# Stacked low-rank products; residual stream loaded behind the branch outputs of the combination, with more load buffers

## The chip, the cores and the metric

The kernel runs on one core of one Trainium2 chip. TensorE (PE in the profile) multiplies matrices into PSUM, VectorE (DVE), ScalarE (ACT) and GpSimd (POOL) work on tiles in SBUF, SyncE (SP) issues the transfers (DMA). The metric is the time of one execution on the device in microseconds.

## The reference

One layer of an encoder with two branches over two batches of 512 tokens, 1024 wide, all in fp32:

```python
h = _rmsnorm(x, norm_mix_g[l])
gates, p_a, pq, pkv, pkr = _split(h @ w_in[l], IN_SPLITS)
p_a = _token_shift(p_a, shift_mu[l])
y_a = _rwkv7_branch(p_a, decay_w2[l], decay_w0[l], iclr_a2[l], iclr_a0[l], gate_g2[l],
                    k_k[l], k_a[l], r_k[l], gn_g[l], gn_b[l]).astype(x.dtype) @ w_oa[l]
y_b = _mla_branch(pq, pkv, pkr, q_norm_g[l], w_uq[l], kv_norm_g[l], w_ukv[l], cos, sin) @ w_ob[l]
g_a, g_b = jnp.split(jax.nn.sigmoid(gates), 2, axis=-1)
x = x + (g_a * y_a + g_b * y_b) @ w_out[l]
h = _rmsnorm(x, norm_ffn_g[l])
gt, up = jnp.split(h @ w_gu[l], 2, axis=-1)
x = x + (jax.nn.silu(gt) * up) @ w_down[l]
```

and a last norm. In the RWKV branch decay and rate come from low-rank products, per direction, with 64 inner rows, and the output gate from one with 160:

```python
wl = -jax.nn.softplus(-(base + jnp.tanh(lora) @ up)) - 0.5
...
return jax.nn.sigmoid(base + lora @ up)
...
g = jax.nn.sigmoid(pg) @ g2
```

## The kernel before

An fp32 product is three matmuls of a rounded type: `split` (L131) makes from a tile a high part (a cast on ACT) and a low part (a subtraction on DVE), and `mm3` adds up high x high, high x low and low x high in one PSUM tile. Nearly all matmuls have 128 rows and 512 columns (a batch's tokens), and are recorded at L125 by `mm`.

In time the program goes: norm and first projections (0 to 50 us); `lora_phase`, with its projections (50 to 160); the latents of attention; the units of RWKV, four head pairs by two batches by two directions, among projections (200 to 700); attention, with the states of the last units (700 to 940); `combine(0)`, the output product of batch 0, `combine(1)` and the output product of batch 1; the norm, the two feed-forward products (1200 to 1813).

`lora_phase` (L404) projects the four low-rank inputs, shifts them along the tokens into `sh` tiles and splits them into `lw`, `la`, `lg`, `lx` (index 0 high, 1 low). For decay and rate both directions share a tile: 64 rows are the one, 64 the other, and the weights `w2` are zero in the rows of the other direction. Then, for each of four pairs `p` and two batches `b`, four products `lu` (decay and rate, two directions) and one `lug` (the gate, in two parts: 128 rows of `lg`, 32 of `lx`) are made in PSUM tiles `mg` (two buffers). A `lu` is evicted by ACT (L464), scaled by POOL (L466) and stored by SP (L467) from a `lut` tile; a `lug` is copied by DVE (L472) and stored. These five share four `lut` buffers.

`combine(b)` (L1034) loads for each pair first the attention output `o_d` (`e` = 1), then the RWKV output `y_d` (`e` = 0) into `ld` tiles (two buffers). To `y_d` POOL adds `bo_d` (L1045) and DVE multiplies the gate (L1046), both loaded into `bg` tiles. Each is split into `yo`. Then for each of eight column blocks `j` it loads `g_` and, for both branches, the weights `wab` into `raw` (two buffers), splits these, and makes the product `pab` of 12 matmuls; a DVE operation multiplies the gate into it (L1062). `pab001` is block 0, batch 0, branch 1, attention.

The residual stream `x2`, eight tiles of 128 tokens by 1024 (512 KB each), is loaded in `combine_thread` (L1099), when all units are done and batch 0's attention is. It is read in the output product.

Two things set the order. TensorE's order is fixed by `drive`: six threads (states, RWKV outputs, solves, preparation, attention, combination) yield, each with a modelled delay, and the first whose time has come goes on; constants such as `YQ`, `YK`, `YO3`, `YS`, `YG`, `L1`, `L2`, `PL` (from a score tile to its transposes `pt`) and `C0` (from the loads to the first `pab`) are such delays. The orders of the other engines and of SP's queue come from the tile scheduler's own simulation. A tile pool's buffer is free for its next tile when its last reader is done.

Names in attention: `sc` are scores, of batch, head and query block (`sc160`: batch 1, head 6, block 0), `mx` and `pr` their minimum and exponential, `pt` the transposes of `pr`, `pT` their copies, `pav` the product with the values, `rbp` its transposes, `rb` the result stored to `o_d`. `rbp_gn13` are the transposes of the last unit's result, behind which stands its store to `y_d`.

Of the kernel before, what the change touches and what calls it, by code (L numbers as in the profile page):

```python
# [19 lines left out]
NB = 2  # L20
# [18 lines left out]
PSTAG = ("f", NF)  # L39
ALAG = 2  # L40
NSTART = 27
L1 = 0.7
L2 = 0.9
L3 = 1.0
TL = 40
SLACK = 1.4
# [10 lines left out]
YP2 = 3  # L57
YP3 = 1
YP4 = 2.84
YG = 0.7  # L60
YT = 1.43
YT2 = 0.85
YM1 = 2
YM2 = 1.1
YO1 = 1.3
YO2 = 2.11
YO3 = 3.44
YS = 0.5
YQ = 2.18
YK = 1.63  # L70
OFFS = 200000, 150000, 120000, 100000, 0, 0
JP = NFF // 2
NRH = 10
# [3 lines left out]
LATW = 0.2  # L77
HOLDW = 0.7
PRIOW = 1
C0 = 18  # L80
PL = 2.81
HORD = (0, 1)
VQB = 3
HALVES = (4,)
# [20 lines left out]
def trunk(ctx, tc, outs, x, w_in, w2, g2, w_uq, w_ukk, w_ukv, w_oab, w_out, w_gu, w_down,  # L105
# [298 lines left out]
    def lora_phase():  # L404
        with ExitStack() as sl:
            lp = pool(sl, "lora")
            lw = [[lp.tile([P, S], F32R, name=f"lw{b}{i}") for i in range(2)] for b in range(NB)]
            la = [[lp.tile([P, S], F32R, name=f"la{b}{i}") for i in range(2)] for b in range(NB)]
            lg = [[lp.tile([P, S], F32R, name=f"lg{b}{i}") for i in range(2)] for b in range(NB)]
            lx = [[lp.tile([P, S], F32R, name=f"lx{b}{i}") for i in range(2)] for b in range(NB)]  # L410
            tosb = lp.tile([64, S], F32, name="tosb")
            nc.sync.dma_start(tosb, to[0:64])
            for b, ps in enumerate((yield from proj(4, "w"))):
                t = sh(f"shw{b}")
                shifted(t, ps, T_W)
                nc.scalar.activation(t, t, AF.Tanh)
                split(*lw[b], t)
            for b, ps in enumerate((yield from proj(5, "a"))):
                t = sh(f"sha{b}")
                shifted(t, ps, T_A)  # L420
                split(*la[b], t)
            for b, ps in enumerate((yield from proj(6, "g"))):
                t = sh(f"shg{b}")
                shifted(t, ps, T_G)
                nc.scalar.activation(t, t, AF.Tanh, scale=0.5)
                nc.vector.tensor_scalar(t, t, 0.5, 0.5, op0=ALU.mult, op1=ALU.add)
                split(*lg[b], t)
            for b, ps in enumerate((yield from proj(3, "x"))):
                t = sh(f"shx{b}")
                nc.vector.memset(t, 0.0)  # L430
                r = slice(64, 96)
                shifted(t, ps, T_X, r)
                nc.scalar.activation(t[r], t[r], AF.Tanh, scale=0.5)
                nc.vector.tensor_scalar(t[r], t[r], 0.5, 0.5, op0=ALU.mult, op1=ALU.add)
                split(*lx[b], t)
                ta, tb = sh(f"kra{b}")[0:32], sh(f"krb{b}")[0:32]
                nc.vector.tensor_mul(ta, ps[0:32], tosb[0:32])
                nc.vector.tensor_mul(tb, ps[32:64], tosb[32:64])
                nc.vector.tensor_add(ta, ta, tb)
                nc.sync.dma_start(kr_d[b][0:32], ta)  # L440
                nc.sync.dma_start(kr_d[b][32:64], ta)
            w2hi = lp.tile([P, 4, S], F32R, name="w2hi")
            w2lo = lp.tile([P, 4, S], F32R, name="w2lo")
            g2hi = lp.tile([P, 2, S], F32R, name="g2hi")
            g2lo = lp.tile([P, 2, S], F32R, name="g2lo")
            for i in range(4):
                t = lp.tile([P, S], F32, tag="raw", bufs=2, name=f"w2raw{i}")
                nc.sync.dma_start(t, w2[i])
                split(w2hi[:, i], w2lo[:, i], t)
            for i in range(2):  # L450
                t = lp.tile([P, S], F32, tag="raw", bufs=2, name=f"g2raw{i}")
                nc.sync.dma_start(t, g2[i])
                split(g2hi[:, i], g2lo[:, i], t)
            for p in range(NPAIR):
                for b in range(NB):
                    sl_p = slice(p * P, (p + 1) * P)
                    for i in range(4):
                        src = lw if i < 2 else la
                        ps = mg(f"lu{b}{p}{i}")
                        yield from mm3(ps, w2hi[:, i, sl_p], w2lo[:, i, sl_p], src[b][0], src[b][1])  # L460
                        t = lp.tile([P, S], F32, tag="lut", bufs=4, name=f"lut{b}{p}{i}")
                        dst = t[:, ::-1] if i % 2 else t
                        hcol = half[:, i * 4 + p:i * 4 + p + 1]
                        nc.scalar.activation(dst, ps, AF.Tanh, scale=0.5, bias=hcol)  # L464
                        f = -0.5 * KAPPA if i < 2 else 0.5
                        nc.gpsimd.tensor_scalar(t, t, f, f, op0=ALU.mult, op1=ALU.add)  # L466
                        nc.sync.dma_start(rwkv_in[b][p][:, 3 + i], t)  # L467
                    ps = mg(f"lug{b}{p}")
                    yield from mm3(ps, g2hi[:, 0, sl_p], g2lo[:, 0, sl_p], lg[b][0], lg[b][1], stop=False)
                    yield from mm3(ps, g2hi[:, 1, sl_p], g2lo[:, 1, sl_p], lx[b][0], lx[b][1], start=False)  # L470
                    t = lp.tile([P, S], F32, tag="lut", bufs=4, name=f"lugt{b}{p}")
                    nc.vector.tensor_copy(t, ps)  # L472
                    nc.sync.dma_start(rwkv_in[b][p][:, 7], t)
        yield from rkv_tiles(0)
# [559 lines left out]
    def combine(b, cp_, newps, m):  # L1034

        yo = [[cp_.tile([P, NPAIR, S], F32R, name=f"yo{b}{e}{j}") for j in range(2)] for e in range(2)]
        for e in (1, 0):
            for p in range(NPAIR):
                t = cp_.tile([P, S], F32, tag="ld", bufs=2, name=f"ld{b}{e}{p}")
                nc.sync.dma_start(t, (y_d, o_d)[e][b][p])  # L1040
                if e == 0:
                    bg = cp_.tile([P, 2, S], F32, tag="g3", bufs=2, name=f"bg{b}{p}")
                    nc.sync.dma_start(bg[:, 0], bo_d[b][p])
                    nc.sync.dma_start(bg[:, 1], rwkv_in[b][p][:, 7])
                    nc.gpsimd.tensor_add(t, t, bg[:, 0])  # L1045
                    nc.vector.tensor_mul(t, t, bg[:, 1])  # L1046
                split(yo[e][0][:, p], yo[e][1][:, p], t)
        yield C0
        for j in range(KD):
            g_ = cp_.tile([P, 2, S], F32, tag="g3", bufs=2, name=f"g3{j}{b}")  # L1050
            nc.sync.dma_start(g_, gate_d[b][j])
            for e in (1, 0):
                raw = cp_.tile([P, 4 * P], F32, tag="raw", bufs=2, name=f"wab{b}{j}{e}")
                nc.sync.dma_start(raw, w_oab[j][:, e * 512:(e + 1) * 512])
                wt = [cp_.tile([P, 4 * P], F32R, tag=f"w{i}", bufs=2, name=f"wab{b}{j}{e}{i}") for i in range(2)]
                split(*wt, raw)
                ps = newps(f"pab{j}{b}{e}")
                for k in range(NPAIR):
                    ws = slice(k * P, (k + 1) * P)
                    yield from mm3(ps, wt[0][:, ws], wt[1][:, ws], yo[e][0][:, k], yo[e][1][:, k],  # L1060
                                   start=(k == 0), stop=(k == NPAIR - 1))
                nc.vector.scalar_tensor_tensor(out=g_[:, e], in0=g_[:, e], scalar=1.0, in1=ps,  # L1062
                                               op0=ALU.add, op1=ALU.mult)
            nc.gpsimd.tensor_add(g_[:, 0], g_[:, 0], g_[:, 1])  # L1064
            nc.scalar.activation(m[0][:, j], g_[:, 0], AF.Copy, scale=0.5)
            nc.vector.scalar_tensor_tensor(out=m[1][:, j], in0=g_[:, 0], scalar=0.5, in1=m[0][:, j],
                                           op0=ALU.mult, op1=ALU.subtract)
# [23 lines left out]
    def combine_thread():  # L1091
        for i in range(NU):
            yield has("post", i)
        yield has("attn", 0)
        rst_.close()
        x2p = pool(p4, "x2p")
        x2.extend(x2p.tile([P, D], F32, name=f"x2_{t}") for t in range(8))
        for t in range(8):
            nc.sync.dma_start(x2[t], x[t // 4, (t % 4) * P:(t % 4 + 1) * P, :])  # L1099
        mtiles(m0st, 0)  # L1100
        with ExitStack() as s3:
            yield from combine(0, pool(s3, "c30"), mg, mt[0])

    done.add(("rkv", 0))
    drive([(100000, first_prep()), (0, latents(latp))])
# [511 lines left out]
def layout(i):  # L1617
# [21 lines left out]
    r["w_in"] = wt.reshape(len(cols), P, KD * P)  # L1639
    w2 = np.zeros((4, P, 512), f)  # L1640
    for d in range(2):
        w2[d, d * 64:(d + 1) * 64] = a["decay_w2"][0, d]
        w2[2 + d, d * 64:(d + 1) * 64] = a["iclr_a2"][0, d]
    r["w2"] = w2
    g2 = np.zeros((2, P, 512), f)
    g2[0] = a["gate_g2"][0, :128]
    g2[1, 64:96] = a["gate_g2"][0, 128:]
    r["g2"] = g2
    uq = a["w_uq"][0].reshape(2, P, 8, 96)
    even = np.concatenate([np.arange(96), 80 + np.arange(16), 64 + np.arange(16)])  # L1650
# [76 lines left out]
```

## Time and profile before

| | |
|---|---|
| median of three runs | 1813.38 us (1812.76 to 1814.93) |
| the profiled execution | 1814.92 us |
| its span, first to last instruction | 1813.1 us |
| mean granted clock of TensorE | 0.981 |
| DMA moved | 208.96 MB, 115 GB/s over the span |

A row of the profile names the line, the engine, the operation and the tiles (written from read). `x48` counts rows, a bracket `[2.53 <-ACT yo L132]` is the idle time ahead of a row and what ended it. A row of a matmul is longer than the distance to the next, since they run on into each other. The granted clock is a share of full speed.

### The profile page before, as it was taken

How to read it: one execution, taken by the hardware profiler on the slowest of the kernel's cores; microseconds unless marked ns; L12 is line 12 of the kernel's file. 1: busy time of each engine (PE TensorE's matmuls, PEld its weight loads, DVE VectorE, ACT ScalarE, POOL GpSimd, SP SyncE). 2: the span in 40 equal slices, each digit the busy share in tenths (PEclk: the TensorE clock that was granted, in tenths of full speed). 3: DMA queues.
4: the chain of work that ended last, by engine and by line, in shares of the span. 5: the costliest groups of instructions: out<-in, count | busy, mean ns of one | idle time of the engine just before them, and what ended most of it. 6: DMA issues, size and time to landing. Idle time of an engine off the chain costs nothing.

```text
span 1813.1 us, 30886 instructions
## 1 busy us (share of the span) xinstructions
PE 1719.7 (95%) x11708; PEld 1359.8 (75%) x11708; DVE 1074.9 (59%) x1773; ACT 778.1 (43%) x1512; POOL 641.4 (35%) x992
## 2 busy tenths in 40 slices
PE   6999989999999997999999999699999999989997
PEld 5887767767777775666667989488888888868886
DVE  6633555635355455765656557956556555488757
ACT  5534343333444335676653324333333333235445
POOL 3012355363644637261012124843333343100006
PEclk8999999999999998999989999899999999999999
DMA  4354433424343334211266641022223222383442
GB/s 158 121 177 163 130 112 90 120 79 130 104 111 107 90 111 113 76 44 45 82 218 210 210 156 36 24 93 95 97 93 105 81 72 91 99 289 123 128 134 93
DMA packets 185332, 208.96 MB, mean 115 GB/s; under 512 B 102816, under 2 KB 114464, under 8 KB 185184
## 3 DMA queue, kind: packets, MB, share of 16 engines
q1 hardware_dynamic: 184320, 205.48, 35.9%
q8 instruction: 92, 1.51, 0.3%
q10 hardware_dynamic: 720, 0.98, 0.2%
q0 software_dynamic: 144, 0.52, 0.1%
q14 instruction: 56, 0.46, 0.1%
HBM read 147.70 MB, written 59.24 MB: 114 GB/s over the span
## 4 chain that ended last, share of the span: by engine, by line
PE 66%; DVE 10%; DMA 9%; POOL 7%; issue 4%; ACT 3%; SPq 1%; DVEq 0%; POOLq 0%; ACTq 0%
PE pgC L125 10%; PE pgB L125 6%; PE pj_gt L125 6%; PE pgA L125 6%; PE dx L125 5%; PE pj_rkv L125 5%; PE dy L125 3%; POOL lt L847 2%; POOL el L849 2%; PE s L125 2%; PE pab L125 2%; PE pj_mla L125 2%; DMA wor<-in_w_out 2%; PE pwo L125 2%; PE gx L125 2%
## 5 line engine op out<-in xcount | busy, mean ns | idle before, releaser
L847 POOL TENSOR_TENSOR lt<-lane,el 128x126 f32<-128x126 f32 (+22 forms) x248 | 96.7, 390 | 38.8 <-DMA lane<-nt_d 20.4
L849 POOL TENSOR_TENSOR el<-el,lt 128x126 f32<-128x126 f32 (+22 forms) x248 | 98.3, 396 | 19.1
L125 PE MATMUL pab<-yo,wab 128*128 128x512 f32 x384 | 97.2, 408 | 7.0 <-ACT yo L132 2.5
L125 PE MATMUL pj_gt<-h_lo,whi_gt 128*128 128x512 f32 x240 | 99.5, 415 | 0.0
L125 PE MATMUL pj_gt<-h_hi,whi_gt 128*128 128x512 f32 x240 | 99.0, 413 | 0.0
L125 PE MATMUL pj_gt<-h_hi,wlo_gt 128*128 128x512 f32 x240 | 98.4, 410 | 0.3 <-DVE wlo_gt L133 0.3
L125 PEld LDWEIGHTS pab<-yo,wab 128*128 128x128 f32 x384 | 73.1, 195 | 28.0 <-DVE wab L133 5.5
L125 PE MATMUL pwo<-woh,m 128*128 128x256 f32 x512 | 93.6, 283 | 0.0
L1217 POOL TENSOR_TENSOR s<-uraw 128x512 f32<-128x512 f32 x22 | 29.3, 1332 | 150.6 <-DMA uraw<-in_w_gu 141.2
L125 PEld LDWEIGHTS pwo<-woh,m 128*128 128x128 f32 x512 | 80.2, 192 | 0.3
L125 PE MATMUL pj_rkv<-h_hi,wlo_rkv 128*128 128x512 f32 x192 | 77.4, 406 | 1.3 <-DVE wlo_rkv L133 1.3
L125 PE MATMUL pj_rkv<-h_hi,whi_rkv 128*128 128x512 f32 x192 | 77.6, 404 | 0.0
L125 PE MATMUL pj_rkv<-h_lo,whi_rkv 128*128 128x512 f32 x192 | 76.7, 399 | 0.0
L125 PE MATMUL pwo<-wol,m 128*128 128x256 f32 x256 | 72.4, 284 | 0.5 <-DVE wol L133 0.5
L1596 POOL TENSOR_TENSOR x<-x,dp 128x512 f32<-128x512 f32 x4 | 6.3, 1591 | 178.8 <-DVE x L1595 178.8
L1285 DVE TENSOR_TENSOR p<-p,pgC 128x512 f32<-128x512 f32 x22 | 15.1, 687 | 86.9 <-PE pgC L125 86.9
L936 ACT COPY sva<-s 64x128 f32<-64x128 f32 x64 | 16.5, 258 | 98.0 <-PE s L125 83.9
L1064 POOL TENSOR_TENSOR g<-g 128x512 f32<-128x512 f32 x16 | 24.2, 1514 | 92.8 <-DVE g L1062 76.0
L937 DVE COPY svb<-s 64x128 f32<-64x128 f32 x64 | 18.8, 294 | 62.3 <-ACT sva L936 33.9
L466 POOL TENSOR_SCALAR lut<-lut 128x512 f32<-128x512 f32 x32 | 20.2, 634 | 98.7 <-ACT lut L464 98.3
L616 DVE TENSOR_REDUCE mx<-sc 128x1 f32<-128x512 f32 x64 | 43.8, 688 | 18.5 <-PE sc L125 17.9
L125 PEld LDWEIGHTS pj_gt<-h_hi,wlo_gt 128*128 128x128 f32 x240 | 45.1, 188 | 9.2 <-DVE wlo_gt L133 1.0
(1561 smaller groups left out, 5533.7 us busy)
## 6 DMA issues: line engine op xcount, KB each, us to landing
graw<-in_w_gu SPq DMA_DIRECT2D x22, 512.0 KB, 3.5
uraw<-in_w_gu SPq DMA_DIRECT2D x22, 512.0 KB, 3.5
a_d<-a SPq DMA_DIRECT2D x21, 512.0 KB, 3.2
w<-in_w_down SPq DMA_DIRECT2D x42, 256.0 KB, 4.3
x<-in_x SPq DMA_DIRECT2D x16, 512.0 KB, 8.0
rwkv_in<-lut SPq DMA_DIRECT2D x32, 256.0 KB, 2.1
gate_d<-gtt SPq DMA_DIRECT2D x32, 256.0 KB, 2.4
wab<-in_w_oab SPq DMA_DIRECT2D x32, 256.0 KB, 3.5
```

What stands on the lines that cost most here:

```text
L125: pin(nc.tensor.matmul(out, lhsT, rhs, start=start, stop=stop, **kw), n if out.shape[0] > 64 else n / 2)
L466: nc.gpsimd.tensor_scalar(t, t, f, f, op0=ALU.mult, op1=ALU.add)
L616: nc.vector.tensor_reduce(mx, sc, axis=AX.X, op=ALU.min)
L847: eng.tensor_mul(lv, lane[:, s, s + 1:].unsqueeze(1).to_broadcast([P, m_, n]), el[:, 0:m_, s].unsqueeze(2).to_broadcast([P, m_, n]))
L849: eng.tensor_add(ev, ev, lv)
L936: nc.scalar.copy(sva[HA, :, c], s2[HA])
L937: nc.vector.tensor_copy(svb[HB, :, c], s2[HB])
L1064: nc.gpsimd.tensor_add(g_[:, 0], g_[:, 0], g_[:, 1])
L1217: vg(ES[min(j, 1)]).tensor_add(s1, a21, a22)
L1285: nc.vector.tensor_add(p1, p1, x_)
L1596: nc.gpsimd.tensor_add(xs(1, t, 1), xs(1, t, 1), p5[t])
```

## The change

It has three parts. In `lora_phase` high and low part of one direction now stand in the two halves of one tile of 128 rows (`stacked`), the weights' 64 rows are laid out twice, and so one matmul makes high x high and low x high: a `lu` has two matmuls instead of three. The 32 rows of the gate's second part become one tile (`lx`, rows 32 to 127: high, high, low) against one weight tile (`g2x`: low, high, high), and `lug` has four matmuls instead of six. In the combination `ld` gets four buffers, `raw` three, `C0` is 14, and the loads of `x2` are written behind the loads of `combine(0)`. Eight delays get other values.

```diff
-L1 = 0.7
-L2 = 0.9
+L1 = 0.55
+L2 = 1.04
-YG = 0.7
+YG = 0.75
-YO3 = 3.44
-YS = 0.5
-YQ = 2.18
-YK = 1.63
+YO3 = 4.26
+YS = 0.41
+YQ = 2
+YK = 1.72
-C0 = 18
-PL = 2.81
+C0 = 14
+PL = 3.5
...
+            top, bot = slice(0, 64), slice(64, 128)
+
+            def stacked(dst, t):
+                for d, (own, other) in enumerate(((top, bot), (bot, top))):
+                    nc.scalar.copy(dst[d][own], t[own])
+                    nc.vector.tensor_sub(dst[d][other], t[own], dst[d][own])
...
-            lx = [[lp.tile([P, S], F32R, name=f"lx{b}{i}") for i in range(2)] for b in range(NB)]
+            lx = [lp.tile([P, S], F32R, name=f"lx{b}") for b in range(NB)]
...
-                split(*lw[b], t)
+                stacked(lw[b], t)
...
-                split(*la[b], t)
+                stacked(la[b], t)
...
-                split(*lx[b], t)
+                for rows, own in ((slice(0, 32), slice(0, 32)), (r, r), (slice(32, 64), r)):
+                    nc.scalar.copy(lx[b][rows], t[own])
+                nc.vector.tensor_sub(lx[b][96:128], t[r], lx[b][r])
...
-                split(g2hi[:, i], g2lo[:, i], t)
+                if i == 0:
+                    split(g2hi, g2lo, t)
+                else:
+                    nc.scalar.copy(g2x[bot], t[bot])
+                    nc.scalar.copy(g2x[0:32], t[0:32])
+                    nc.vector.tensor_sub(g2x[32:64], t[64:96], g2x[64:96])
...
-                        yield from mm3(ps, w2hi[:, i, sl_p], w2lo[:, i, sl_p], src[b][0], src[b][1])
+                        mm(ps, w2hi[:, i, sl_p], src[b][i % 2], stop=False)
+                        yield 0
+                        mm(ps, w2lo[:, i, sl_p], src[b][i % 2], start=False)
+                        yield 0
...
-                    yield from mm3(ps, g2hi[:, 0, sl_p], g2lo[:, 0, sl_p], lg[b][0], lg[b][1], stop=False)
-                    yield from mm3(ps, g2hi[:, 1, sl_p], g2lo[:, 1, sl_p], lx[b][0], lx[b][1], start=False)
+                    yield from mm3(ps, g2hi[:, sl_p], g2lo[:, sl_p], lg[b][0], lg[b][1], stop=False)
+                    mm(ps, g2x[:, sl_p], lx[b], start=False)
+                    yield 0
...
-                t = cp_.tile([P, S], F32, tag="ld", bufs=2, name=f"ld{b}{e}{p}")
+                t = cp_.tile([P, S], F32, tag="ld", bufs=4, name=f"ld{b}{e}{p}")
...
-                raw = cp_.tile([P, 4 * P], F32, tag="raw", bufs=2, name=f"wab{b}{j}{e}")
+                raw = cp_.tile([P, 4 * P], F32, tag="raw", bufs=3, name=f"wab{b}{j}{e}")
...
-        for t in range(8):
-            nc.sync.dma_start(x2[t], x[t // 4, (t % 4) * P:(t % 4 + 1) * P, :])
         mtiles(m0st, 0)
         with ExitStack() as s3:
-            yield from combine(0, pool(s3, "c30"), mg, mt[0])
+            cg = combine(0, pool(s3, "c30"), mg, mt[0])
+            yield next(cg)
+            for t in range(8):
+                nc.sync.dma_start(x2[t], x[t // 4, (t % 4) * P:(t % 4 + 1) * P, :])
+            yield from cg
...
-        w2[d, d * 64:(d + 1) * 64] = a["decay_w2"][0, d]
-        w2[2 + d, d * 64:(d + 1) * 64] = a["iclr_a2"][0, d]
+        w2[d] = np.tile(a["decay_w2"][0, d], (2, 1))
+        w2[2 + d] = np.tile(a["iclr_a2"][0, d], (2, 1))
...
-    g2[1, 64:96] = a["gate_g2"][0, 128:]
+    g2[1, 64:] = np.tile(a["gate_g2"][0, 128:], (2, 1))
```

In TensorE's order, near the end of `lora_phase`, before (the last `lu` of pair 3, batch 0, and its `lug`):

```order
L125 MATMUL lu033_1073<-la00_385,w2hi_769 128x512
L125 MATMUL lu033_1073<-la01_386,w2hi_769 128x512
L125 MATMUL lu033_1073<-la00_385,w2lo_770 128x512
L125 MATMUL lug03_1081<-lg00_389,g2hi_771 128x512
L125 MATMUL lug03_1081<-lg01_390,g2hi_771 128x512
L125 MATMUL lug03_1081<-lg00_389,g2lo_772 128x512
L125 MATMUL lug03_1081<-lx00_393,g2hi_771 128x512
L125 MATMUL lug03_1081<-lx01_394,g2hi_771 128x512
L125 MATMUL lug03_1081<-lx00_393,g2lo_772 128x512
```

The same place after the change:

```order
L125 MATMUL lu033_1046<-la01_386,w2hi_779 128x512
L125 MATMUL lu033_1046<-la01_386,w2lo_780 128x512
L125 MATMUL lug03_1053<-lg00_389,g2hi_781 128x512
L125 MATMUL lug03_1053<-lg01_390,g2hi_781 128x512
L125 MATMUL lug03_1053<-lg00_389,g2lo_782 128x512
L125 MATMUL lug03_1053<-lx0_393,g2x_783 128x512
```

Three matmuls became two and six became four; `la01` is now the stacked tile of the second direction. TensorE has 48 rows fewer in all.

SP's queue where the residual stream is loaded, before (`x2_4` is its fifth tile, `ld010` the first load of the combination, `wab011` a weight tile, `o_d11` a store of attention):

```order
L1099 DMA x2_4_10374<-in_x 128x1024
L1099 DMA x2_5_10375<-in_x 128x1024
L1099 DMA x2_6_10376<-in_x 128x1024
L1099 DMA x2_7_10377<-in_x 128x1024
L1040 DMA ld010_10398<-o_d00_99 128x512
L575 DMA o_d11_104<-rb11_10363 128x512
L1040 DMA ld011_10402<-o_d01_100 128x512
L1043 DMA bg00_10416<-bo_d00_122 128x512
L1044 DMA bg00_10416<-rwkv_in00_75 128x512
L1054 DMA wab011_10847<-in_w_oab 128x512
L1054 DMA wab010_10867<-in_w_oab 128x512
L1043 DMA bg01_10425<-bo_d01_123 128x512
```

The same positions of the queue after the change:

```order
L1122 DMA x2_4_10287<-in_x 128x1024
L1122 DMA x2_5_10288<-in_x 128x1024
L1059 DMA ld010_10303<-o_d00_99 128x512
L1122 DMA x2_6_10289<-in_x 128x1024
L1122 DMA x2_7_10290<-in_x 128x1024
L1059 DMA ld011_10307<-o_d01_100 128x512
L1073 DMA wab001_10552<-in_w_oab 128x512
L1073 DMA wab000_10676<-in_w_oab 128x512
L1073 DMA wab011_10755<-in_w_oab 128x512
L1059 DMA ld012_10311<-o_d02_101 128x512
L1059 DMA ld013_10315<-o_d03_102 128x512
L1062 DMA bg00_10321<-bo_d00_122 128x512
```

Two of the eight `x2` loads moved behind `ld010`; six still stand ahead of it, although they are written behind it. `wab001` and `wab000`, which stood ahead of `x2_0` before, now stand behind `ld011`, and `o_d11` behind the `ld` loads of branch 1.

TensorE's order at the end of attention, before:

```order
L129 MATMUL pt151_10578<-idn_62,pr151_10515 128x128 x4
L125 MATMUL sc160_10586<-kt100_9626,qh16_10532 128x512
L125 MATMUL sc160_10586<-kt101_9627,qh16_10532 128x512
L125 MATMUL sc160_10586<-kt100_9626,ql16_10533 128x512
L129 MATMUL pt152_10595<-idn_62,pr152_10548 128x128 x4
L125 MATMUL sc161_10601<-kt100_9626,qh16_10532 128x512
L125 MATMUL sc161_10601<-kt101_9627,qh16_10532 128x512
L125 MATMUL sc161_10601<-kt100_9626,ql16_10533 128x512
```

The same place after the change:

```order
L129 MATMUL pt151_10534<-idn_62,pr151_10471 128x128 x4
L125 MATMUL pab001_10558<-yo010_10301,wab0010_10554 128x512
L125 MATMUL pab001_10558<-yo011_10302,wab0010_10554 128x512
L125 MATMUL pab001_10558<-yo010_10301,wab0011_10555 128x512
L125 MATMUL sc160_10562<-kt100_9620,qh16_10488 128x512
L125 MATMUL sc160_10562<-kt101_9621,qh16_10488 128x512
L125 MATMUL sc160_10562<-kt100_9620,ql16_10489 128x512
L129 MATMUL pt152_10571<-idn_62,pr152_10504 128x128 x4
```

The first matmuls of `pab001` moved from behind `sc170` to behind `pt151`. The last row of `pab000`, which reads the last `yo` of batch 0, stood behind `rbp13` before and stands ahead of `pt172` now; ahead of `rbp13` there were 18 rows of `pab` and are 31. Earlier in attention `rbp_gn13` stood behind `pt132` before and stands ahead of `pt130` now.

More of the change, by code (lines that the diff above doesn't have):

```diff
@@ L443, in lora_phase @@
             w2lo = lp.tile([P, 4, S], F32R, name="w2lo")
-            g2hi = lp.tile([P, 2, S], F32R, name="g2hi")
-            g2lo = lp.tile([P, 2, S], F32R, name="g2lo")
+            g2hi = lp.tile([P, S], F32R, name="g2hi")
+            g2lo = lp.tile([P, S], F32R, name="g2lo")
+            g2x = lp.tile([P, S], F32R, name="g2x")
             for i in range(4):
```

## The prediction

> **What bounds the kernel now.** First the page: how busy each engine is, and what the chain that ended last is made of.
>
> ```profile
> PE 1719.7 (95%) x11708; PEld 1359.8 (75%) x11708; DVE 1074.9 (59%) x1773; ACT 778.1 (43%) x1512; POOL 641.4 (35%) x992
> PE 66%; DVE 10%; DMA 9%; POOL 7%; issue 4%; ACT 3%; SPq 1%; DVEq 0%; POOLq 0%; ACTq 0%
> ```
>
> TensorE holds two thirds of the chain, so a matmul taken out counts where TensorE never waits, and elsewhere only as far as what it waits for comes earlier too. 95% is an average, so the two changed stages are read apart, each with the view of busy time by stretches (start:end, length, then busy time and count for PE, PEld, DVE, ACT and POOL, the granted clock, DMA share, GB/s). First the low-rank stage:
>
> ```profile
> 50.00:75.00 25.00, 25.00 (x111) 20.63 (x110) 15.70 (x25) 13.80 (x24) 2.75 (x4) 1.00 0.41 137
> 75.00:100.00 25.00, 25.00 (x111) 20.51 (x111) 16.81 (x25) 9.69 (x16) 2.48 (x4) 1.00 0.36 118
> 100.00:125.00 25.00, 25.00 (x111) 20.49 (x110) 8.45 (x13) 9.70 (x15) 4.47 (x7) 1.00 0.50 156
> 142.00:160.00 18.00, 17.14 (x74) 11.93 (x72) 2.33 (x4) 8.25 (x12) 7.44 (x12) 1.00 0.55 214
> ```
>
> Up to 125 us TensorE is busy all the time, with 111 matmuls of 512 columns in 25 us: **25/111 = 0.225 us from start to start**, at full clock (the 0.39 us of a single row overlaps its neighbours). There a removed matmul is worth its 0.225. From 142 on there are gaps, and the timeline of PE shows their pattern:
>
> ```profile
> 144.19 0.62 PE L125 MATMUL lu<-lw,w2hi 128*128 128x512 f32 x2
> ...
> 145.19 0.72 PE L125 MATMUL lu<-lw,w2hi 128*128 128x512 f32 x2 [0.16 <-DVE lugt L472]
> ...
> 149.16 0.62 PE L125 MATMUL lu<-lw,w2hi 128*128 128x512 f32 x2
> ...
> 154.14 0.61 PE L125 MATMUL lu<-lw,w2hi 128*128 128x512 f32 x2
> ```
>
> The last three blocks stand back to back, one in (154.14 - 144.19) / 2 = 4.98 us, while their 18 matmuls need 18 x 0.225 = 4.05. TensorE waits there for the eviction, through the two `mg` buffers.
>
> The other stage is the start of combine(0). The timeline of PE, rows with a wait ahead of them:
>
> ```profile
> 932.64 0.50 PE L125 MATMUL pab<-yo,wab 128*128 128x512 f32 x1 [0.66 <-DVE yo L133]
> ...
> 942.08 3.23 PE L125 MATMUL pab<-yo,wab 128*128 128x512 f32 x6 [2.53 <-ACT yo L132]
> 945.84 14.42 PE L125 MATMUL pab<-yo,wab 128*128 128x512 f32 x50 [0.54 <-DVE g L1062]
> 961.13 3.06 PE L125 MATMUL pab<-yo,wab 128*128 128x512 f32 x12 [0.87 <-DVE wab L133]
> 964.63 5.25 PE L125 MATMUL pab<-yo,wab 128*128 128x512 f32 x22 [0.45 <-DVE wab L133]
> 970.93 1.45 PE L125 MATMUL pab<-yo,wab 128*128 128x512 f32 x4 [1.05 <-ACT wab L132]
> ```
>
> The waits for `yo` and the gate product come to 0.66 + 2.53 + 0.54 = 3.73 us, those for `wab` to 2.37. Behind the longest the matmuls are also slow: six take 3.23 us and fifty 14.42, where at 0.225 they would take 1.35 and 11.25. The stretches say why:
>
> ```profile
> 940.00:945.00 5.00, 2.92 (x6) 1.78 (x6) 3.87 (x5) 1.79 (x4) 0.83 (x1) 0.64 0.52 170
> 945.00:950.00 5.00, 4.46 (x11) 3.29 (x11) 2.58 (x4) 1.16 (x2) 1.61 (x1) 0.50 0.59 208
> 950.00:955.00 5.00, 5.00 (x20) 4.03 (x19) 3.24 (x6) 2.38 (x4) 0.00 (x0) 0.83 0.95 340
> ```
>
> The granted clock is down to half for about 10 us. That costs (3.23 - 1.35) + (14.42 - 11.25) = 5.05, less about 0.4 for the two row ends that run on: **4.6 us**.
>
> **Why `yo` is late.** Busy transfers of 900 to 915, the residual stream's eight loads (L1099, start of the first and last), and what belongs to the tiles `ld`:
>
> ```profile
> 905.00:910.00 5.00, 5.00 (x28) 4.12 (x27) 2.78 (x5) 3.66 (x11) 0.00 (x0) 1.00 1.03 415
> 910.00:915.00 5.00, 4.21 (x24) 2.99 (x23) 3.83 (x8) 4.89 (x12) 0.00 (x0) 1.00 1.04 398
> ...
> L1099 SPq DMA_DIRECT2D x<-in_x x8: 382/529/924, 898.3 to 902.6; - x8
> ...
> L132 ACT CAST yo<-ld x8: 617/620/632, 915.4 to 942.0; 128x512 fp32r<-128x512 f32 x8
> L133 DVE TENSOR_TENSOR yo<-ld,yo x8: 678/688/693, 916.1 to 942.7; 128x512 fp32r<-128x512 f32 x8
> L1040 SPq DMA_DIRECT2D ld<-o_d x4: 319/320/326, 904.5 to 919.1; - x4
> L1040 SPq DMA_DIRECT2D ld<-y_d x4: 319/320/422, 924.9 to 934.0; - x4
> L1045 POOL TENSOR_TENSOR ld<-ld,bg x4: 1260/1272/1284, 927.7 to 939.6; 128x512 f32<-128x512 f32 x4
> L1046 DVE TENSOR_TENSOR ld<-ld,bg x4: 676/1206/1760, 929.0 to 941.3; 128x512 f32<-128x512 f32 x4
> ...
> DMA to landing us min/median/max: 2.6/4.1/9.6
> ```
>
> The transfers run full (share 1.03) while eight loads of 512 KB, 1.27 us each at 412 GB/s, come ahead of the first `ld`, issued at 904.5 and landed 9.6 us later, about 914.1. With two `ld` buffers the y_d loads then wait for splits of o_d tiles and are issued from 924.9 on; the last split starts at 942.7.
>
> **The change, part by part.**
>
> *Stacked products.* Per pair and batch 18 matmuls become 4 x 2 + 3 + 1 = 12, over eight blocks 48 fewer. 3 x 6 = 18 of these lie in the last three blocks, the other 30 where TensorE is busy all the time (nearly: two in the last `lug` ahead of them): 30 x 0.225 = **6.8 us**. In the last blocks the bound is the eviction, from these rows of the tile `lut`, 140 to 162:
>
> ```profile
> L466 POOL TENSOR_SCALAR lut<-lut x14: 617/619/628, 139.6 to 158.7; 128x512 f32<-128x512 f32 x14
> L467 SPq DMA_DIRECT2D rwkv_in<-lut x14: 319/320/368, 140.2 to 159.3; - x14
> L464 ACT ACTIVATE lut<-lu,half x13: 687/687/698, 139.3 to 157.9; 128x512 f32<-128x512 f32 x13
> ...
> DMA to landing us min/median/max: 2.0/2.0/3.0
> ```
>
> A buffer is held for 0.69 + 0.62 + 2.0 = 3.3 us and some tenths of handing over, say 3.5, a `lugt` (no POOL step) some 2.8; five tiles over four buffers make (4 x 3.5 + 2.8) / 4 = 4.2 a block. I take 4.3. Ends: ACT alone, 4 x 0.69 = 2.75, and no gain, 4.98. So 3 x (4.98 - 4.3) = **2.0 us**, between 0 and 6.7. The stage gives 8.8, between 6.8 and 13.5.
>
> The stacking adds 9 casts on ACT and 4 subtractions on DVE; fewer rows make them no cheaper:
>
> ```profile
> L439 DVE TENSOR_TENSOR kra<-kra,krb 32x512 f32<-32x512 f32 x2 | 1.4, 678 | 0.1
> L132 ACT CAST la<-sha 128x512 fp32r<-128x512 f32 x2 | 1.2, 616 | 0.0
> ```
>
> 9 x 0.62 + 4 x 0.68 = 8.3 us, which I cost at nothing: between 50 and 125 TensorE has projections queued, DVE is idle for at least 8 of each 25 us and ACT for 11. If that cover went, 8.3 would come back and the stage would be 1.5 us worse than none at all on its low end; the rows exclude that while projections stand between the products.
>
> *Loads of the combination.* By SP's order six of the eight residual loads still stand ahead of the first `ld`, not none. What changes: two loads and the two weight loads fewer ahead of it (2 x 1.27 + 2 x 0.64 = 3.8 us), and all of it starts earlier, since `rbp_gn13` now stands ahead of `pt130` instead of behind `pt132`:
>
> ```profile
> 890.22 0.60 PE L129 MATMUL pt<-idn,pr 128*128 128x128 f32 x4
> ...
> 894.61 0.66 PE L129 MATMUL rbp_gn<-idn,rb_gn 128*128 128x128 f32 x4
> ```
>
> That is 4.4 us. So the first `ld` lands near 914.1 - 3.8 - 4.4 = 906 on the old clock, and ACT casts it right behind the exponential of `pr150`, near 909. With four buffers the y_d loads no longer wait for `o_d12`'s store or for splits; I place the first at 914 and, with 4.1 to land, 1.27 for POOL's sum, about 1.2 for the product, twice over for the ring of two `bg` tiles, 0.62 and 0.69 for the split, the last `yo` at 929, instead of 942.7. Its first reader on TensorE stands near 931. So the 3.73 go, and with the long wait the half clock, 4.6. For later `wab`, with three buffers instead of two, I take half of the 2.37: 1.2. Against it: the matmuls of `pab001` stand earlier, behind `pt151`, while `wab001` is now loaded behind the `ld`s; TensorE can wait there, and once more for the last `yo`. Ends: 0 and the 2.53 that it waits today; I take 1.5 for both together, nearer to the long end since the margins are 2 us or less. Queued behind such a wait are `sc160`, `pt152` and `qps17`, hence ACT's copies. **3.73 + 4.6 + 1.2 - 1.5 = 8.0 us**, between 0 (the loads' order decides) and 3.73 + 4.6 + 2.37 = 10.7.
>
> *The constants* move rows in the units by a few places, and in attention put the transposes `pt` about one piece later. TensorE waits there little:
>
> ```profile
> PE pt L129 <- ACT pr L618: 1.7, 4, 0.7
> PE pt L129 <- ACT pT L555: 1.0, 2, 0.8
> ```
>
> 2.7 us in six waits is all that later transposes can win; the same again may be lost. I take 0.
>
> *Sum:* 8.8 + 8.0 = 16.8 us. The profiled execution took 1814.92, so 1798.1; the median of the three runs, 1813.38, lies 1.54 lower, so **1796.6**.
>
> **The rivals.**
>
> *Six loads ahead are as bad as eight* (the change doesn't do what it says). If the earlier start doesn't come about, the first `ld` lands near 910, ACT stands at its cast ahead of `pr151`, and what the y_d side wins is lost to exponentials. For it: SP's order and the share of 1.03. Against: it is y_d, not o_d, that ends last. Only the 8.8 remain: 1804.6.
>
> *The half clock stays.* [...] Then 4.6 of the 8.0 are missing, the sum is 12.2, the time 1801.2. [...]
>
> *More is won:* the last blocks go at ACT's 2.75 (4.7 more) and the 2.7 of `pt` vanish: 1789.2. Against it: the landing of 2.0 us is in the ring.
>
> *Attention stalls (slower).* The new order lets each of the 64 pieces wait once for its exponential or its copy, because the casts of `yo` and `wab` now stand in ACT's queue between them and state rows are moved. The six waits above average 0.45 us; 64 x 0.45 = 29 us, so 1825.4. It decides from 16.8 / 64 = 0.26 us a piece on. Against: transposes stand later, not earlier, and only the last ten pieces share ACT with the casts.
>
> **How the numbers follow.** Forecast 0.62, six loads as bad 0.12, half clock stays 0.14, more 0.06, attention stalls 0.06. A measurement of this kernel tells about 0.2% (3.6 us) from no change. The first four are faster by more: 0.94. Of the stalls 0.04 are slower, 0.02 land within 0.2%. The range goes from 1789.5, near the two upper ends together (13.5 + 10.7 = 24.2, 1789.2), to 1805.5, just beyond the case of the six loads.
>
> **What would show it.** Right: 48 matmuls fewer and `ss_kk` about 8.8 us earlier; blocks of `lu` 4.3 us apart at the end; the last `yo` split about 11 us before the old place, no wait for `yo` over 1 us, clock 1.00 through the start of combine(0). Wrong: TensorE waiting in 50 to 125; a half clock behind a wait for `wab001` or `yo`; many small waits at `pt` or `sc` between 705 and 930; a dip that has moved to the norm ahead of the feed-forward part.

## The result, and the profile after

| | before | after |
|---|---|---|
| median | 1814.16 us (1812.76 to 1816.37, 4 runs) | 1801.62 us (1799.46 to 1804.07, 4 runs) |
| ratio, 95% interval | | 0.9923 (0.991 to 0.9935) |
| the profiled execution | 1814.92 us | 1804.07 us |
| its span, mean clock | 1813.1 us, 0.981 | 1802.3 us, 0.980 |

The kernel became faster by 12.5 us in the medians, 11.8 to 16.3 by the interval of the ratio. The forecast was 16.8 less and 1796.6 us, with a range of 1789.5 to 1805.5. The profiled execution after is the slowest of the four; the other three had clocks of 0.983, 0.981 and 0.983 at 1799.46, 1802.57 and 1800.66 us.

The page after, busy time by engine and the chain:

```profile
PE 1713.5 (95%) x11660; PEld 1353.0 (75%) x11660; DVE 1080.5 (60%) x1777; ACT 784.4 (44%) x1521; POOL 639.8 (35%) x992
PE 69%; DVE 9%; DMA 7%; POOL 6%; issue 6%; ACT 3%; SPq 1%; POOLq 0%; DVEq 0%; ACTq 0%
```

48 matmuls are gone, and the clock is no better. The start of combine(0) after, by the tile `ld` (first and last start) and by stretches (the granted clock is the third number from the end):

```profile
L132 ACT CAST yo<-ld x8: 617/628/647, 906.1 to 928.5; 128x512 fp32r<-128x512 f32 x8
L133 DVE TENSOR_TENSOR yo<-ld,yo x8: 682/690/1726, 907.5 to 930.8; 128x512 fp32r<-128x512 f32 x8
L1059 SPq DMA_DIRECT2D ld<-o_d x4: 326/326/472, 895.7 to 904.1; - x4
L1059 SPq DMA_DIRECT2D ld<-y_d x4: 319/322/326, 909.4 to 918.4; - x4
...
940.00:945.00 5.00, 5.00 (x25) 4.19 (x25) 2.47 (x4) 1.83 (x3) 0.00 (x0) 1.00 0.35 115
945.00:950.00 5.00, 4.82 (x22) 3.65 (x20) 2.52 (x5) 1.51 (x3) 1.61 (x1) 1.00 0.89 271
```

The clock is full where it was half, as forecast, and no row waits for `yo` any more. The times are further from the forecast than they look. Its 909 for the first cast and 929 for the last split were on the clock of before, and attention now begins 6.5 us earlier (first `kps` at 698.7 instead of 705.2). Counted from there, the first cast came 2.8 us earlier than before (207.4 instead of 210.2; 6.4 were forecast) and the last split 5.4 us earlier (232.1 instead of 237.5; 13.7 were forecast). The timeline of PE has one new wait, the one expected at the earlier `pab001`, and later waits for weights and for the gate product:

```profile
911.84 1.31 PE L125 MATMUL pab<-yo,wab 128*128 128x512 f32 x3 [0.85 <-ACT wab L132]
...
950.84 6.09 PE L125 MATMUL pab<-yo,wab 128*128 128x512 f32 x24 [1.02 <-ACT wab L132]
957.50 17.72 PE L125 MATMUL pab<-yo,wab 128*128 128x512 f32 x76 [0.58 <-DVE g L1081]
```

The last blocks of the low-rank stage are what was not forecast. The timeline of PE:

```profile
135.61 0.39 PE L125 MATMUL lu<-lw,w2hi 128*128 128x512 f32 x1
...
139.78 0.44 PE L125 MATMUL lu<-lw,w2hi 128*128 128x512 f32 x1
...
145.13 0.39 PE L125 MATMUL lu<-lw,w2hi 128*128 128x512 f32 x1
...
149.26 0.50 PE L125 MATMUL lu<-la,w2hi 128*128 128x512 f32 x1 [1.64 <-ACT lut L482]
...
151.72 1.70 PE L125 MATMUL ss_kk<-blk2sb,kksq 128*128 128x2 f32 x8
```

They take 4.17, 5.35 and 6.59 us, 16.1 together, where 14.9 stood before and 12.9 were forecast; from 149.8 on the clock is half (0.50) for 6.8 us. The waiting engine is ACT, whose evictions wait for stores to land (timeline of ACT):

```profile
141.79 1.34 ACT L482 ACTIVATE lut<-lu,half 128x512 f32<-128x512 f32 x2 [2.12 <-DMA rwkv_in<-lut]
...
148.53 1.27 ACT L482 ACTIVATE lut<-lu,half 128x512 f32<-128x512 f32 x2 [1.68 <-DMA rwkv_in<-lut]
```

In these blocks before the change, stores issued 0.7 to 1.1 us after each other mostly landed after 2.0 us. After it, five are issued within 2.9 us from 143.2 on (3.6 us or more before), and two of them took 3.65 and 3.61 us, so the ring turned more slowly just when it should turn faster. That closeness alone lengthens them is argued, not shown: other stores, 0.7 to 1.1 us apart, took 2.8 us here.

To see where time went, the span is cut at the starts of the first rows of `pj_a` (the low-rank stage), `gx` (the units), `kps` (attention), `pwo` (the output product) and `nt_f` (norm and feed-forward). Microseconds of the profiled executions, up to the end of the last matmul (the 7.8 to 7.9 us of the span behind it are left out), with three of the experiments below:

| stage | before | after | stack only | buffers only | stack and loads |
|---|---|---|---|---|---|
| ahead of `pj_a` | 42.8 | 41.1 | 41.8 | 42.9 | 42.7 |
| low-rank stage, latents | 155.0 | 152.5 | 148.0 | 155.0 | 148.1 |
| units | 507.4 | 505.3 | 508.8 | 508.3 | 508.6 |
| attention, combine(0) | 286.1 | 280.9 | 283.2 | 277.2 | 276.3 |
| output product to combine(1) | 103.7 | 102.3 | 104.9 | 102.3 | 102.3 |
| from the norm on | 710.2 | 712.5 | 710.0 | 712.5 | 712.5 |

The low-rank stage is 4.5 us longer after the change than with the products alone. In it 13.7 us stand at half clock after and 3.4 with the products alone; half of the difference, 5.1 us by an estimate, would account for it.

### The profile page after: what moved, and what is told of

Read it like the earlier page. It is cut to its first block, busy times and chain, and to the rows that moved or that the text cites. A ratio compares the mean times of both kernels' runs of the same rounds, so it can differ in the third digit from the quotient of the medians.

```text
span 1802.3 us, 30805 instructions
## 1 busy us (share of the span) xinstructions
PE 1713.5 (95%) x11660; PEld 1353.0 (75%) x11660; DVE 1080.5 (60%) x1777; ACT 784.4 (44%) x1521; POOL 639.8 (35%) x992
## 4 chain that ended last, share of the span: by engine, by line
PE 69%; DVE 9%; DMA 7%; POOL 6%; issue 6%; ACT 3%; SPq 1%; POOLq 0%; DVEq 0%; ACTq 0%
PE pgC L125 10%; PE pj_gt L125 8%; PE pgB L125 7%; PE pgA L125 6%; PE dx L125 4%; PE pab L125 4%; PE pwo L125 4%; PE s L125 3%; PE dy L125 2%; PE sc L125 2%; POOL el L868 2%; POOL lt L866 2%; PE pav L125 2%; PE gx L125 2%; PE dz L125 2%
## 5 line engine op out<-in xcount | busy, mean ns | idle before, releaser
L125 PE MATMUL pab<-yo,wab 128*128 128x512 f32 x384 | 91.3, 393 | 2.6 <-ACT wab L132 1.9
```

The source lines that it names most:

```text
L125: pin(nc.tensor.matmul(out, lhsT, rhs, start=start, stop=stop, **kw), n if out.shape[0] > 64 else n / 2)
```

## The experiments

Each was timed against the kernel before. Two theories on the whole stood against each other: that the three parts add up, with the low-rank stage's gain cut by the ring of `lut`; or that they work only together.

**The products alone.** The changed kernel with the old loads, `C0` and delays.

> The stacked low-rank products alone, with the old loads and constants. Theory A (from the trace after): the 28 matmuls taken out while TensorE is busy bring 6.3 us, but the last three blocks are bound by the four lut buffers and their stores, so they stay at 5 us or more each, and the waits bring a half clock behind them; in all 2 to 4 us less than before (1810 to 1812 on 1814). Theory B (the prediction): the last blocks go at 4.3 us, in all 8.8 less (1805).

1806.36 us on 1814.23, ratio 0.9964 (0.9952 to 0.9976). The low-rank stage is 7.0 us shorter, 6.9 of it before the last three blocks begin. These blocks take 4.17, 5.40 and 5.70 us, the last two as theory A has it, but no half clock follows, so the time lies between the theories. The wait is nearly the same as in the whole change:

```profile
149.96 0.50 PE L125 MATMUL lu<-la,w2hi 128*128 128x512 f32 x1 [1.51 <-ACT lut L482]
```

**The loads alone.**

```diff
-C0 = 18
+C0 = 14
...
-                t = cp_.tile([P, S], F32, tag="ld", bufs=2, name=f"ld{b}{e}{p}")
+                t = cp_.tile([P, S], F32, tag="ld", bufs=4, name=f"ld{b}{e}{p}")
...
-                raw = cp_.tile([P, 4 * P], F32, tag="raw", bufs=2, name=f"wab{b}{j}{e}")
+                raw = cp_.tile([P, 4 * P], F32, tag="raw", bufs=3, name=f"wab{b}{j}{e}")
...
-        for t in range(8):
-            nc.sync.dma_start(x2[t], x[t // 4, (t % 4) * P:(t % 4 + 1) * P, :])
...
-            yield from combine(0, pool(s3, "c30"), mg, mt[0])
+            cg = combine(0, pool(s3, "c30"), mg, mt[0])
+            yield next(cg)
+            for t in range(8):
+                nc.sync.dma_start(x2[t], x[t // 4, (t % 4) * P:(t % 4 + 1) * P, :])
+            yield from cg
```

> The combination's loads alone (four ld buffers, three for the weights, residual loads written behind, C0 of 14), with the old products and delays; TensorE's order is that of before. Theory A: the waits for yo (3.7 us) and the half clock behind them (4.6 us) go, 8 to 9 us less (1805 to 1806). Theory B (six residual loads ahead are as bad as eight): first yo cast behind 912, last yo behind 938, the half clock stays, under 2 us less.

1807.71 us, ratio 0.9964 (0.9951 to 0.9977). Attention with combine(0) falls from 286.1 to 279.2, the stage to combine(1) from 103.7 to 102.3: 8.3 us, as theory A says. The median gained 6.5 us, less than theory A's 8 to 9 and far more than theory B's 2.

**The buffers alone**: of the diff above the two lines of `ld` and of `raw`.

> The kernel before with four ld and three raw buffers, all eight residual loads still ahead of the first ld. Theory A (the buffers carry the gain of the loads, since it is y_d that ends last): last yo before 936, no half clock at 941, 5 to 7 us less than before (1807 to 1809). Theory B (the residual loads' place carries it): within 2 us of before.

1807.33 us on 1814.07, ratio 0.9957 (0.9944 to 0.9971): as much as all the loads together. What `raw` has in it was not timed by itself. The tile `ld` of this run:

```profile
L132 ACT CAST yo<-ld x8: 616/630/690, 917.3 to 936.1; 128x512 fp32r<-128x512 f32 x8
L133 DVE TENSOR_TENSOR yo<-ld,yo x8: 682/684/905, 918.0 to 937.8; 128x512 fp32r<-128x512 f32 x8
L1040 SPq DMA_DIRECT2D ld<-o_d x4: 319/320/326, 906.4 to 911.6; - x4
L1040 SPq DMA_DIRECT2D ld<-y_d x4: 319/320/320, 918.8 to 922.9; - x4
```

TensorE waits for none of the `yo`: 937.8 is early enough for the old order. The run before this one differs from it by the residual loads' place and `C0` alone. Counted from the first `kps` (702.9 there, 706.2 here), the first cast comes at 205.8 us there and at 211.1 here, so the place brings it 5.3 us. The last split starts at 231.5 and 231.6: there the place brings nothing.

The reason stands in SP's queue. Eight loads share four buffers, so the `y_d` loads still wait for splits of `o_d` tiles, each for the split four tiles earlier. SP's waits in the trace after the change (us in all, times, longest), from 905 to 935, where L1059 issues the `y_d` loads alone:

```profile
SPq L1059 <- DVE yo L133: 5.3, 3, 2.1
```

Three of the four loads wait for a split, and the last `yo` follows these splits, not the first cast.

**The residual loads back in front**, the rest as in the changed kernel.

> The changed kernel with the residual loads written ahead of combine(0), as before the change; SP's order has all eight ahead of the first ld again. Theory A (the buffers alone carry the gain): within 2 us of the changed kernel (1800 to 1804); the first yo cast up to 3 us later, its wait at the first pab 1 to 3 us longer. Theory B (the place matters with the new order of attention): 5 us or more slower (1807 or more).

1803.48 us on 1814.69, ratio 0.9938 (0.9924 to 0.9951), against 0.9923 for the whole change: theory A. Counted from the first `kps` (701.0 here), the first `yo` is cast 3.2 us later than in the changed kernel (210.6 instead of 207.4), and the last split starts as early (232.2 and 232.1); the place of the residual loads is worth nothing that these runs can tell.

**Two `ld` buffers**, the rest as in the changed kernel.

```diff
-                t = cp_.tile([P, S], F32, tag="ld", bufs=4, name=f"ld{b}{e}{p}")
+                t = cp_.tile([P, S], F32, tag="ld", bufs=2, name=f"ld{b}{e}{p}")
```

> The changed kernel with two ld buffers instead of four; the order of TensorE at the end of attention stays the changed one. Theory A (the new order puts 31 pab rows ahead of the last pav and rbp, and pays only while yo is early; without the buffers their waits stand in attention): the last yo behind 940, waits for yo ahead of the last pav, in all 6 us or more slower than the changed kernel (1808 to 1823). Theory B (the residual loads' new place makes the order pay): 1800 to 1804.

1807.79 us, ratio 0.9965 (0.9953 to 0.9977): 6.2 us of the gain gone, by theory A, though the last split started at 935.4 and not behind 940. In the new order that is too late; waits of PE in this run:

```profile
934.10 0.51 PE L125 MATMUL pab<-yo,wab 128*128 128x512 f32 x1 [3.00 <-ACT yo L132]
935.25 1.22 PE L125 MATMUL pab<-yo,wab 128*128 128x512 f32 x2 [0.65 <-DVE yo L133]
```

They stand ahead of the last `pav` and `rbp`, and a half clock begins at 935.0.

**The delays alone**: `L1`, `L2`, `YG`, `YO3`, `YS`, `YQ`, `YK` and `PL` as in the changed kernel, all else as before.

> The eight modelled delays alone (order of TensorE in the units and in attention), old products and loads. Theory A: the delays cost what attention lost in the trace after; from the first kps to the last rbp it takes 2 to 4 us longer than before's 234.1, after taking off 0.23 us for each pab row more ahead of the last rbp, and in all the kernel is 0 to 4 us slower. Theory B: the delays are worth nothing by themselves (within 1.5 us both ways in that stretch), and attention lost its time to the casts of yo that now stand in ACT's queue.

1830.7 us, ratio 1.0091 (1.0078 to 1.0104): 16.5 slower, far more than either theory. From the first `kps` to the last `rbp` it takes 254.5 us instead of 234.1, with 6 `pab` rows (1.4 us) more. The waits for `yo` now stand inside attention:

```profile
949.91 0.50 PE L125 MATMUL pab<-yo,wab 128*128 128x512 f32 x1 [2.64 <-ACT yo L132]
951.13 0.50 PE L125 MATMUL pab<-yo,wab 128*128 128x512 f32 x1 [0.73 <-DVE yo L133]
...
954.11 1.22 PE L125 MATMUL pab<-yo,wab 128*128 128x512 f32 x2 [1.01 <-DVE yo L133]
```

**The delays with the buffers**, to split these 16.5 us: the same, with four `ld` and three `raw`.

> The kernel before with the eight new delays and with four ld and three raw buffers: the run of the delays alone plus the buffers, nothing else; 24 pab rows stand ahead of the last rbp, as there. Theory A (two causes in the 16.5 us of the delays alone: some 7 to 10 us of waits for yo ahead of the last pav, which the buffers cure, and some 6 to 8 us lost between 690 and 915, which they don't): 1820 to 1824. Theory B (the late yo is all of it): 1807 to 1810, as with the buffers alone. Theory C (yo has no part in it): 1828 or more.

1819.14 us on 1814.25, ratio 1.0026 (1.0015 to 1.0036), a little below theory A's band. So the buffers took away 11.6 of the 16.5, and 4.9 remain. The waits for `yo` shown above come to 4.4 us and a half clock of 6.8 us behind them, at 951.8, to 3.4 by an estimate; both are gone, and the rest of the 11.6 was not traced. Against the buffers alone (6.7 us less than before) the delays cost 11.6 here, although `yo` is early. Two waits of the states, 4.21 us at 717 and 2.21 at 733, have half clocks behind them, where the changed kernel waits 2.02 us; why the states wait there without the stacked products and not with them was not settled.

**Products and loads, old delays.**

> The changed kernel with the eight old delays: stacked products and the combination's loads alone. Theory A (parts add up): the median gains 7.9 and 6.5 of the two alone make 14.4, so about 1800 on 1814, at or below the whole change; attention from the first kps to the last rbp takes 230 to 235 us as in the kernel before. Theory B (the new delays are what makes the loads pay): above 1804.

1801.5 us on 1814.07, ratio 0.993 (0.9918 to 0.9942): the same as the whole change, so no gain or loss of the delays can be told in its company. Theory B falls; by theory A 14.4 were expected and 12.6 came. This trace has a half clock of 3.4 us in combine(0), at 944.5, behind a wait of 1.83 us for `wab`: with the wait for `yo` gone, the half clock stands here behind another wait of the stage.

**Half of the delays each**: only those of the units, then only those of attention.

> The changed kernel with the old delays of attention (PL, YQ, YK), so the new ones only in the units (L1, L2, YG, YO3, YS). Theory A (the attention delays cost, the unit delays win): the waits near 650 to 667 stay gone (2 to 3 us), attention takes 230 to 235 us, about 1797. Theory B (it is the unit delays that lengthen attention, by moving the last states): attention 238 or longer, 1802 or more.

> The changed kernel with the old delays of the units, so the new ones only in attention (PL, YQ, YK). Theory A: attention takes 239 to 243 us (of which 2.9 are the 13 pab rows more ahead of the last rbp), waits near 650 to 667 are back, about 1804. Theory B: attention 230 to 236 us, about 1798.

1801.13 us (0.9922, 0.991 to 0.9935) and 1806.09 us (0.9956, 0.9944 to 0.9969). Attention from the first `kps` to the last `rbp` takes 234.7 and 244.3 us: the attention delays lengthen it, as theory A says (244.3 is above its band, and both times are 2 to 4 us above those that theory A named). The waits near 650 to 667, 2.6 us before, are nearly gone in both (0.0 and 0.4 us), but so they are with the products alone (0.0) and not with the loads or the buffers alone (2.1 and 1.6). They went with the stacked products, not with the delays, and the units did not become shorter by it (508.6 and 509.0).

**Six `lut` buffers**, the rest as in the changed kernel.

```diff
-                        t = lp.tile([P, S], F32, tag="lut", bufs=4, name=f"lut{b}{p}{i}")
+                        t = lp.tile([P, S], F32, tag="lut", bufs=6, name=f"lut{b}{p}{i}")
...
-                    t = lp.tile([P, S], F32, tag="lut", bufs=4, name=f"lugt{b}{p}")
+                    t = lp.tile([P, S], F32, tag="lut", bufs=6, name=f"lugt{b}{p}")
```

> The changed kernel with six lut buffers instead of four; nothing else differs, and all engines keep their order. Theory A (the lut ring bounds the last blocks): they go at 2.8 to 3.3 us instead of 4.2 to 6.6, no half clock at 150, 8 to 10 us less than the changed kernel (about 1792 where before is 1814). Theory B (the stores' bandwidth or ACT bounds them): blocks stay over 4 us and the time within 3 us of the changed kernel's.

1800.73 us, ratio 0.9925 (0.9911 to 0.9938): no gain that can be told, by theory B's number. The blocks take 4.20, 4.46 and 5.00 us, so the ring was the long part of the wait, but behind it TensorE still waits for the evictions of its two `mg` tiles (timeline of PE in this run):

```profile
139.47 0.50 PE L125 MATMUL lu<-la,w2hi 128*128 128x512 f32 x1 [0.37 <-ACT lut L482]
...
143.95 0.51 PE L125 MATMUL lu<-la,w2hi 128*128 128x512 f32 x1 [0.66 <-ACT lut L482]
```

**Six `lut` and `lug` in the `f` tiles**, on the kernel with the unit delays only.

```diff
-                    ps = mg(f"lug{b}{p}")
+                    ps = pf(f"lug{b}{p}")
```

> As e7 (changed kernel, attention delays of before), with six lut buffers and with lug in the PSUM tiles f (four buffers) instead of mg, so that the last blocks have six lut and an extra PSUM tile. Theory A (ring of lut and two mg tiles together bound the last blocks): blocks of 3.0 to 3.6 us, 3 to 5 us less than e7 (1796 to 1798). Theory B (stores or ACT bound them): blocks stay above 4 us, within 2 us of e7.

1805.79 us, ratio 0.9952 (0.9939 to 0.9965), slower than its base. It doesn't decide between the theories: the scheduler moved the blocks among the projections, where TensorE then waited 5.6 us (0.0 before) and ran at half clock at 85.5. No version beat the changed kernel by what can be measured.

## Why the prediction was right, and where it was off

*Matmuls while TensorE is busy.* 30 x 0.225 = 6.8 us was forecast; from the first `pj_a` to the first of the last three blocks it was 6.9 us less in the trace after (94.5 against 101.4). The extra casts and subtractions cost nothing there, as argued: no gap on PE in 50 to 125.

*The last blocks.* Forecast 4.3 us each and 2.0 in all; measured 16.1 against 14.9, a loss of 1.2 (with the products alone 15.3). The mechanism named, a ring of four `lut`, was right for the long waits (ACT waits 2.12 and 1.68 us for stores), but its period was mis-sized: I took the landing of 2.0 us as fixed, and it grew to as much as 3.65. It is also not the only bound: with six `lut` the blocks still take 4.20 to 5.00 us. This term is off by 2.3 to 3.2 us.

*Loads of the combination.* Forecast 8.0, with the bound from the last `yo`; 8.3 us in the two stages of the run with the loads alone, 6.5 in its median. What was named as lost, the waits for `yo` and the half clock behind them, went. The way to it failed in two steps, and that the first cast fell on 906.1, near the forecast's 909, is luck, since that was on the clock of before.

The first step is the 4.4 us for `rbp_gn13`. Its rows and the first `kps`, after the change:

```profile
698.74 1.22 PE L125 MATMUL kps<-lat,wkh 128*128 128x512 f32 x2 [4.54 <-ACT wkh L132]
...
889.15 0.60 PE L129 MATMUL rbp_gn<-idn,rb_gn 128*128 128x128 f32 x4
889.59 0.60 PE L129 MATMUL pt<-idn,pr 128*128 128x128 f32 x4
```

From the first `kps` to this `pt130` it takes 190.9 us, before 185.0 (890.22 - 705.2). The new order did move `rbp_gn13` ahead of `pt130`, but attention had become 5.9 us longer up to there, so it came at 190.4 instead of 189.4. The second step is the sentence that with four buffers the `y_d` loads no longer wait for splits: three of four do. So the last split came 5.4 us earlier and not 13.7, and the 3.8 us that were credited to the residual loads and the weights, of which 3.2 came at the first cast, are worth nothing at the last one. The buffers alone bring the last `yo` ahead of its readers, because 2.53 us and a little more was all that was missing. The rival of the six loads named the reason, that it is `y_d` that ends last, and still gave the loads' place the whole of the 8.0. Unforecast: 1.4 us in the stage to combine(1).

*The half clock.* 4.6 us were credited for the dip at 941. It went, in the changed kernel too, and the rival in which it stays, whose 1801.2 is by chance almost the measured time, did not happen. But the mean clock did not rise: 0.981 before, 0.980 after, with new dips at 149.8, 259.0, 835.9 and 1784.8. A dip taken out at one place was booked as a gain of the whole, while others came elsewhere. The four runs after show the size: 0.980 and 1804.07 us at one end, 0.983 and 1799.46 at the other. From the norm on, where the change does nothing, 2.3 us were lost in the profiled execution, where 27.3 us stand at half clock instead of 23.9.

*The delays.* Forecast 0, and none that can be told in the sum (ratios 0.9923 with, 0.993 without). Behind it stands a size that I did not see: attention and combine(0) are 4.6 us longer than without the new delays (280.9 against 276.3). The units are 3.3 us shorter in these two traces, but this is not shown to be the delays' gain: with the residual loads back in front and the same delays they take 511.2. What makes up for the 4.6 in the medians stays open. The slower rival named the stage, not the mechanism: there is no wait at each piece (0.5 + 0.3 us in all at `pt` after). The delays by themselves cost 16.5 us, 4.9 with the buffers, and nothing that can be told with the buffers and the stacked products; only a part of it is `yo` being late for its readers.

In all: 6.9 as forecast; 2.3 to 3.2 missing in the last blocks; 1.5 missing where the loads alone gave 6.5 for 8.0. That is about the 4.3 by which 12.5 falls short of 16.8. The forecast of the time was right, but the sum fits better than its terms: the last blocks lost where a gain was forecast, and the combination's gain came by another way than was argued. Differences of this size lie within the runs' spread of 4.6 us.

## What to carry to other kernels

When matmuls are taken out, look at the last stretch in which they stand back to back: what bounded it here was the ring behind them, and its slowest part, the landing of stores, did not stay as it was when it was driven faster (2.0 us before, up to 3.65 after). Test a move of loads against the buffers alone; the earlier load is worth nothing if another tile of the same group ends last, and with buffers shared by both groups the later loads still wait for the work on the earlier ones (5.3 us in three waits here). When a forecast names a time in the trace, count it from a row near by, or the gain of an earlier stage passes for its own. An order that costs nothing with early data can cost much when the data is late, so an order and the buffers that it rests on are to be timed together and apart. And a half clock removed at one place is not to be counted as a gain of the whole before the mean clock shows it (0.981 before and 0.980 after here).

## What the runs showed of the hardware

In the traces before and after, every edge of a dip of the granted clock, except at the program's end, lies on a grid of 3.413 us (0.001 us off at most), and the two grids, counted from the first instruction, are 0.28 us apart. The clock is 1.00 or 0.50 in each stretch between two lines of the grid. From the first record of the clock to the last matmul, 2 of the 981 full stretches of these two traces in which TensorE was idle for less than 45% were followed by a half one (one in each trace, at 180.3 and 177.1 us, where mostly matmuls of one column run); of those with 45 to 55% it was 5 of 9; of those above, 15 of 15. Of the half stretches with less than 15% idle, 21 of 23 were followed by a full one, of the others 1 of 16. What sets the clock was not shown, only these counts. Stretches cut on this grid, of the trace before:

```profile
938.02:941.43 3.41, 1.52 (x8) 0.47 (x5) 1.79 (x2) 0.02 (x1) 2.48 (x2) 1.00 0.07 25
941.43:944.85 3.42, 2.77 (x6) 1.78 (x6) 2.44 (x4) 1.69 (x3) 0.00 (x0) 0.50 0.71 230
```

of the trace after, in the last blocks of the low-rank stage:

```profile
146.40:149.82 3.42, 1.75 (x6) 0.62 (x5) 0.00 (x0) 1.71 (x3) 1.15 (x2) 1.00 0.57 218
149.82:153.23 3.41, 3.41 (x13) 3.00 (x13) 0.69 (x1) 0.69 (x1) 1.33 (x3) 0.50 0.60 231
```

and of the run with the products alone, at the same place in the program:

```profile
148.23:151.64 3.41, 1.90 (x8) 1.14 (x8) 0.00 (x0) 2.01 (x3) 1.52 (x4) 1.00 0.47 183
151.64:155.06 3.42, 3.42 (x21) 2.96 (x21) 0.86 (x2) 0.95 (x2) 2.13 (x2) 1.00 0.74 286
```

Busy for 1.75 us of the stretch, TensorE fell to half clock for the next 6.8 us; busy for 1.90, it did not, after a wait that was only 0.13 us shorter. That the length of a wait alone does not tell whether a dip follows shows in attention, where TensorE waits 1.6 us for `kt` in the trace after and as long in the run with the residual loads back in front. In the trace after the wait lies within one stretch, and a half one follows:

```profile
832.48:835.90 3.42, 1.82 (x23) 1.25 (x21) 3.31 (x8) 2.67 (x6) 0.80 (x2) 1.00 0.05 16
835.90:839.31 3.41, 3.41 (x24) 2.58 (x25) 1.71 (x4) 0.47 (x2) 0.00 (x0) 0.50 0.00 0
```

In the run with the residual loads back in front a line of the grid cuts it in two, and no half stretch follows:

```profile
834.26:837.67 3.41, 1.91 (x22) 1.29 (x22) 3.29 (x7) 2.91 (x6) 0.80 (x2) 1.00 0.07 19
837.67:841.08 3.41, 3.30 (x34) 2.43 (x35) 2.53 (x6) 1.52 (x4) 0.00 (x0) 1.00 0.00 0
```

At a clock of 0.50 a stretch of 3.41 us that is busy all the time loses half of itself, so by an estimate from these rows the same wait costs nothing more, or some 1.7 us more for each half stretch behind it. The dip at 941 stands right behind a stretch that was idle for 1.89 of its 3.41 us, by its row above, and all of this lies in the wait for `yo` that ends at 942.08.
